# RWKV-7 decode states in a one-core hybrid decoder step: the sample's state update in transposed form

## The chip, the cores and the metric

The kernel runs on one NeuronCore of a Trainium2 chip. The metric is the device time of one execution in microseconds (us). PE is the matrix engine, PEld its weight loads, DVE the vector engine, ACT the scalar engine, POOL the general-purpose engine (which also issues stores and gathers), SP the engine that issues most loads.

## What is computed

One layer of a decoder works on a prompt (1 x 512 tokens) and on a sample group (8 sequences of 4 new tokens). A projection `z = RMSNorm(x) @ W_in` is cut into an RWKV-7 group (4 heads of 64), an attention group with forget gates (FoX, 8 heads, for the sample over 2048 paged tokens of the past) and a convolution group. Their outputs go through `W_out`, then come a cross attention and a feed-forward part. The RWKV group carries a state S per sequence and head (64 x 64, value v by key k); for the sample it is read, stepped four times and written back as `s_rwkv`:

```
def step(S, inp):
    r_t, w_t, k_t, v_t, kk_t, a_t = inp
    sa = jnp.einsum('bhvk,bhk->bhv', S, -kk_t)
    S = S * w_t[:, :, None, :] + sa[..., None] * (kk_t * a_t)[:, :, None, :] + v_t[..., None] * k_t[:, :, None, :]
    return S, jnp.einsum('bhvk,bhk->bhv', S, r_t)
```

## The kernel before

The kernel is one program of unrolled instructions. It is written as Python generators whose steps are woven by assumed costs (`woven`, L330); a scheduler then orders the instructions of every engine at build time, by data, by free buffers and by place in the program. `tc.high_priority(800)` moves what is issued under it 800 places ahead. An engine runs its list strictly in that order.

Up to about 320 us of the span three streams are woven (L1244): `fox_and_conv`, the rest of the input projection (products of 128x128 weights with 272 columns in fp32r, three per weight block, into `bank_g`); `rwkv_recurrence`, urgent by 800 (L1243); and `conv_ahead`. The first of them ends the stretch; what is left of the others is issued in `rest` (L1583), which goes on with `recurrence_end` (L1281: two ACT passes, then L1286 and L1287 on POOL, over the RWKV output), the prompt's attention, the memory keys and values, and the output projection of the prompt. Beside `rest` runs `sample_past` (L1708), the attention of the sample over its past: for every sequence four gathers of keys (1 MB each, issued by POOL), transposed by DVE (L1407) into `KT`, and four gathers of values into `page`.

`sample_steps` (L968) is the last part of `rwkv_recurrence`. It works on 32 sample tokens per head (8 sequences by 4), which lie on 32 partitions per head (`po`), while keys and values of a head lie on 64 partitions (`ro`):

- L969 to L979: the state is loaded with v on the partitions (two loads of 256 KB), then turned to k on the partitions (`S0T`) by 32 products with the identity. A float32 product is two PE instructions, a transposition (`tr`, L214) one.
- L983 to L988: `TKs` gets the token-major forms of four sources (`beta`, `kap`, `zv`, `e3s`) by 16 products.
- L989 to L1031: the small triangular systems of the four steps, and the products of `S0T` with r and kk (L1017), 512 columns wide on 64 rows. They end in the updated values `Un` (L1033).
- L1034 to L1048: the output y, its group norm, its transposition (L1045) and the sum into `ynT`, which `recurrence_end` takes.
- L1051 to L1067: the new state in the first orientation. POOL spreads three rows of `TKs` over the 8 sequences (L1054, in `two`, which takes the place of `S0T`, and `sel_t`). For each of two j, and each of its two heads, three products of 32 rows by 64 weights by 512 columns follow: `Un` by spread keys, `TKs[.., 2]` by spread keys, and ones by the spread decay (`e3s`), the last to copy the decay to all rows of v. DVE adds and multiplies from PSUM (L1064, L1065), and two stores of 256 KB leave by POOL.

All PSUM tiles of this part come from `rb(k)` (L373), three banks with one buffer each: a tile on bank k waits until the last one there has been read. The prompt's attention takes the same three banks (`xb`, L1253) afterwards.

Of the kernel before, what the change touches and what calls it, by code (L numbers as in the profile page):

```python
# [8 lines left out]
F32 = mybir.dt.float32  # L9
# [11 lines left out]
NB = 8  # L21
TS = 4
# [132 lines left out]
def hybrid_step(tc, A):  # L155
# [20 lines left out]
    def acopy(out, in_):  # L176
        nc.scalar.copy(out, in_)  # L177
# [7 lines left out]
    def mm(out, lhsT, rhs, start=True, stop=True):  # L185
        pinned(nc.tensor.matmul(out, lhsT, rhs, start=start, stop=stop, skip_group_check=True))  # L186
# [9 lines left out]
    def C(name, lo=0, n=None):  # L196
        o, w = _CF[name]
        o -= 128
        return cf[:, o + lo: o + (w if n is None else lo + n)]
# [309 lines left out]
    for h4 in range(2):  # L509
        ps = xb()  # L510
# [385 lines left out]
    def rwkv_recurrence():  # L896
# [71 lines left out]
        def sample_steps(rk, rk2):  # L968
            S0 = rk.tile([128, 2, NB, 64], F32, name="S0")  # L969
            for j in range(2):  # L970
                load(out=S0[:, j], in_=A["state_rwkv"][0, :, 2 * j: 2 * j + 2].rearrange("b r v k -> (r v) b k"))
            S0T = rk.tile([128, 2, NB, 64], F32, name="S0T")
            for j in range(2):
                ps = rb(j)
                for b in range(NB):
                    for r in range(2):
                        ro = HALF[r]
                        mm(ps[ro, b * 64: b * 64 + 64], S0[ro, j, b], ident[ro, ro])
                acopy(S0T[:, j], ps.rearrange("p (b v) -> p b v", v=64))  # L979
# [3 lines left out]
            TKs = rk.tile([128, 4, 64], F32, name="TKs")  # L983
            ps = rb(2)
            for n, src in enumerate((beta, kap, zv, None)):
                for h, j, po, ro in HR:
                    mm(ps[po, n * 64: n * 64 + 64], e3s[ro, j] if src is None else src[ro, j, sm], ident[ro, ro])
            acopy(TKs, ps[:, :256].rearrange("p (n v) -> p n v", v=64))  # L988
# [36 lines left out]
            for h, j, po, ro in HR:  # L1025
                mm(ps[po, 0:64], GS[po, 96:128], TKs[po, 2])
            rhs = rk.tile([128, 64], F32, name="rhs")
            vtt(out=rhs, in0=ps[:, 0:64], in1=sel[0], op=ADD)
            for h, j, po, ro in HR:
                mm(ps[po, 64:128], RS[po], rhs[po])  # L1030
            yield 2.0  # L1031
            Un = rk.tile([128, 64], F32, name="Un")
            vcp(Un, ps[:, 64:128])  # L1033
            for h, j, po, ro in HR:  # L1034
                mm(ps[po, 128:192], GS[po, 0:32], Un[po], True, False)
            for h, j, po, ro in HR:
                mm(ps[po, 128:192], GS[po, 64:96], TKs[po, 2], False, True)
# [13 lines left out]
            two = rk.tile([128, 2, NB, 64], F32, name="S0T")  # L1051
            ex = [two[:, 0], two[:, 1], rk2.tile([128, NB, 64], F32, name="sel_t")]
            for n, (src, m) in enumerate(((0, "own"), (1, "own"), (3, "last"))):
                ptt(out=ex[n], in0=TKs[:, src, None, :].broadcast_to([128, NB, 64]), in1=C(m)[:, :, None].broadcast_to([128, NB, 64]), op=MUL)  # L1054
            for j in range(2):
                ps, ps2 = rb(0), rb(1)
                for r in range(2):
                    h = 2 * j + r
                    po, ro = HR[h][2], HR[h][3]
                    mm(ps[ro, :], Un[po], ex[0][po], True, False)  # L1060
                    mm(ps[ro, :], TKs[po, 2], ex[1][po], False, True)
                    mm(ps2[ro, :], ones[po, :64], ex[2][po])
                S0j = S0[:, j].rearrange("p b k -> p (b k)")
                vtt(out=S0j, in0=ps, in1=S0j, op=ADD)  # L1064
                vtt(out=S0j, in0=ps2, in1=S0j, op=MUL)  # L1065
            for j in range(2):
                store(out=A["s_rwkv"][0, :, 2 * j: 2 * j + 2].rearrange("b r v k -> (r v) b k"), in_=S0[:, j])  # L1067

# [1133 lines left out]
```

## Time and profile before

| what | us |
|---|---|
| runs of the kernel | 1249.62, 1257.96, 1259.0; median 1257.96 |
| the profiled execution | 1254.13 |
| its span, first to last instruction | 1252.2 |
| mean granted clock of PE | 0.959 of full |

The profile gives one execution. The span leaves out 1.9 us at the ends. Times in the rows are microseconds from the span's start where not marked ns. PEclk is the clock granted to PE as a share of full speed (1.00 is 2.4 GHz, 0.50 is 1.2 GHz). In rows of instructions, "32*64 32x512" is a weight of 32 rows and 64 columns with 512 columns streamed, and "x8" a count.

### The profile page before, as it was taken

Reading aid. Unit: us, or ns where it says so; the run is one execution under the profiler, and the core shown is the slowest. Engines: PE = TensorE matmul, PEld = TensorE weight load, DVE = VectorE, ACT = ScalarE, POOL = GpSimd, SP = SyncE. Lnnn points to the kernel's source line nnn. Section 1 sums busy time; section 2 is a strip of 40 time slices with the busy share of each in tenths; the row PEclk is TensorE's granted clock in tenths of the full one; section 3 lists DMA queues with packets and bytes.
Section 4 is the critical chain, followed back from the end, with each engine's and each line's share of the span. In section 5 each row is a group of like instructions: output and inputs, shape, how many; then the busy total and the mean of one; then the engine's idle time right before and its main releaser. Section 6 shows DMA issues by size and latency. Waiting matters only on the chain.

```text
span 1252.2 us, 24836 instructions
## 1 busy us (share of the span) xinstructions
PE 1162.3 (93%) x10410; PEld 996.7 (80%) x10410; DVE 808.3 (65%) x1516; ACT 500.2 (40%) x994; POOL 288.4 (23%) x322
## 2 busy tenths in 40 slices
PE   6889989999899998988989879999999999999997
PEld 6788878884655566775569756999999999999996
DVE  4798998865578666783345766567777325767522
ACT  5454543341346553432433333254444223444321
POOL 1252430132533322312322330031111001111120
PEclk9999999997688998989989999999999999999998
DMA  7222220131677799979425462232321332322241
GB/s 236 62 68 53 52 77 2 54 94 39 204 288 282 273 338 360 336 257 304 169 91 161 131 247 72 77 121 70 100 91 57 97 91 95 102 90 70 81 126 35
DMA packets 129650, 173.83 MB, mean 139 GB/s; under 512 B 7030, under 2 KB 110982, under 8 KB 121337
## 3 DMA queue, kind: packets, MB, share of 16 engines
q1 hardware_dynamic: 88160, 70.76, 18.6%
q0 software_dynamic: 15216, 84.80, 18.5%
q10 hardware_dynamic: 26160, 16.66, 4.7%
q8 instruction: 82, 1.34, 0.5%
q14 instruction: 32, 0.25, 0.1%
HBM read 164.54 MB, written 7.88 MB: 138 GB/s over the span
## 4 chain that ended last, share of the span: by engine, by line
PE 46%; issue 7%; DVE 4%; DMA 3%; ACT 2%; POOL 1%; POOLq 0%; DVEq 0%; ACTq 0%
PE bank_g L186 33%; PE bank_d L186 7%; PE bank_s L186 2%; PE bank_a L186 2%; PE bank_v L186 1%; DMA page<-in_cache_fox_v_dram,kidx 1%; PE bank_t L216 1%; DVE w_lo L247 1%; DMA w_raw<-in_cache_fox_k_dram,kidx 1%; ACT w_hi L177 1%; DVE KT L1407 1%; DMA w_raw<-in_w_xq_dram 0%; DMA w_raw<-in_w_xo_dram 0%; DVE four L1649 0%; PE bank_r L186 0%
## 5 line engine op out<-in xcount | busy, mean ns | idle before, releaser
L186 PE MATMUL bank_g<-four,w_hi 128*128 128x272 f32 (+1 forms) x1536 | 278.0, 299 | 4.9 <-ACT w_hi L177 4.3
L177 ACT CAST w_hi<-w_raw 128x1024 fp32r<-128x1024 f32 (+3 forms) x149 | 140.5, 946 | 264.2 <-PE bank_g L186 189.2
L186 PEld LDWEIGHTS bank_g<-four,w_hi 128*128 128x128 f32 x1536 | 222.1, 189 | 14.5 <-issue 5.1
L247 DVE TENSOR_TENSOR w_lo<-w_raw,w_hi 128x1024 fp32r<-128x1024 f32 (+3 forms) x149 | 163.6, 1099 | 81.8 <-ACT w_hi L177 74.2
L186 PE MATMUL bank_g<-four,w_lo 128*128 128x272 f32 (+1 forms) x768 | 172.0, 299 | 0.0
L186 PE MATMUL bank_g<-act_h,w_hi 128*128 128x272 f32 (+2 forms) x400 | 123.8, 309 | 5.9 <-ACT w_hi L177 2.0
L186 PEld LDWEIGHTS bank_g<-four,w_lo 128*128 128x128 f32 x768 | 122.0, 189 | 5.5 <-issue 2.9
L186 PE MATMUL bank_g<-act_l,w_hi 128*128 128x272 f32 (+2 forms) x400 | 121.1, 303 | 0.0
L186 PE MATMUL bank_g<-act_h,w_lo 128*128 128x272 f32 (+2 forms) x400 | 120.8, 302 | 0.0
L2113 POOL TENSOR_SCALAR ysm<-HS,vec 128x32 f32<-128x32 f32 x44 | 42.0, 955 | 255.1 <-ACT HS L177 255.1
L186 PEld LDWEIGHTS bank_g<-act_h,w_hi 128*128 128x128 f32 x400 | 78.4, 196 | 11.5 <-issue 3.8
L186 PEld LDWEIGHTS bank_g<-act_l,w_hi 128*128 128x128 f32 x400 | 78.5, 196 | 2.7 <-issue 1.2
L1407 DVE STREAM_TRANSPOSE KT<-w_raw 128x2048 f32<-128x2048 f32 x32 | 73.6, 2301 | 10.9 <-DMA w_raw<-in_cache_fox_k_dram,kidx 9.9
L186 PEld LDWEIGHTS bank_g<-act_h,w_lo 128*128 128x128 f32 x400 | 78.0, 195 | 1.3 <-issue 0.2
L186 PE MATMUL bank_d<-four,w_hi 128*128 128x272 f32 x384 | 78.4, 300 | 0.0
L186 PE MATMUL bank_g<-in_h,w_hi 128*128 128x272 f32 x352 | 73.5, 290 | 0.0
L186 PE MATMUL bank_g<-in_l,w_hi 128*128 128x272 f32 x352 | 73.5, 290 | 0.0
L186 PE MATMUL bank_g<-in_h,w_lo 128*128 128x272 f32 x352 | 73.4, 289 | 0.0
L186 PEld LDWEIGHTS bank_d<-four,w_hi 128*128 128x128 f32 x384 | 62.1, 193 | 0.9
L2105 DVE TENSOR_TENSOR up<-bank_g,tot 128x544 f32<-128x544 f32 x44 | 31.8, 722 | 44.3 <-PE bank_g L186 44.3
L186 PE MATMUL bank_d<-four,w_lo 128*128 128x272 f32 x192 | 56.8, 296 | 0.0
L1392 POOL DMA_INDIRECT w_raw<-in_cache_fox_k_dram,kidx x32 | 34.2, 1069 | 97.1 <-DVE KT L1407 64.1
(632 smaller groups left out, 2425.7 us busy)
## 6 DMA issues: line engine op xcount, KB each, us to landing
w_raw<-in_w_up_dram SPq DMA_DIRECT2D x20, 1024.0 KB
w_raw<-in_w_down_dram SPq DMA_DIRECT2D x16, 704.0 KB
w_raw<-in_w_in_dram SPq DMA_DIRECT2D x17, 512.0 KB
w_raw<-in_cache_mem_k_dram SPq DMA_DIRECT2D x16, 512.0 KB
sV<-in_cache_mem_v_dram POOLq DMA_DIRECT2D x12, 512.0 KB
w_raw<-in_w_in_dram SPq DMA_DIRECT2D x4, 1024.0 KB
w_raw<-in_w_xk_dram ACTq DMA_DIRECT2D x8, 512.0 KB
w_raw<-in_w_xv_dram ACTq DMA_DIRECT2D x8, 512.0 KB
```

What stands on the lines that cost most here:

```text
L177: nc.scalar.copy(out, in_)
L186: pinned(nc.tensor.matmul(out, lhsT, rhs, start=start, stop=stop, skip_group_check=True))
L216: pinned(nc.tensor.transpose(out=out, in_=in_, identity=ident[p0:p0 + k, p0:p0 + k]))
L247: tt(out=l, in0=src, in1=h.bitcast(F32), op=SUB)
L1392: nc.gpsimd.indirect_dma_start(out=t, out_offset=None, in_=A[cache][0].rearrange("n (k j) h d -> (n k) (j h d)", j=4), in_offset=bass.Indi ...
L1407: nc.vector.transpose(out=KT, in_=K)
L2105: vtt(out=two(x[:, 2:]), in0=ev2(ps), in1=two(rstd), op=MUL)
L2113: nc.gpsimd.tensor_scalar(out=ysm, in0=H[:, 2:6, 1:], scalar1=w[2], scalar2=b, op0=MUL, op1=ADD)
```

## The change

The state stays in the transposed form `S0T` (k on the partitions) until the end. The loads bring two sequences side by side on the partitions, four heads along the free axis, so that 8 transpositions of 128x128 replace the 32 products. `TKs` holds v, and beneath each other beta (32 rows) and kap (32 rows) for two heads. `Un` and v are built a second time, beneath each other in the same order (`below`), and spread over the sequences by DVE (`ex`). One product of 64 rows by 64 weights by 512 columns per head, four in all, then gives the sum of both outer products. DVE adds it to `S0T` and multiplies by the decay, which in this orientation is a number per partition and sequence, straight from `e3s`. Eight transpositions and two ACT copies bring the state back, and 8 stores of 64 KB write it.

```diff
         def sample_steps(rk, rk2):
-            S0 = rk.tile([128, 2, NB, 64], F32, name="S0")
-            for j in range(2):
-                load(out=S0[:, j], in_=A["state_rwkv"][0, :, 2 * j: 2 * j + 2].rearrange("b r v k -> (r v) b k"))
+            S0 = rk.tile([128, 4, 256], F32, name="S0")
+            for b in range(NB):
+                load(out=S0[HALF[b % 2], b // 2].rearrange("p (h k) -> p h k", k=64), in_=A["state_rwkv"][0, b].rearrange("h v k -> v h k"))
             S0T = rk.tile([128, 2, NB, 64], F32, name="S0T")
             for j in range(2):
                 ps = rb(j)
-                for b in range(NB):
-                    for r in range(2):
-                        ro = HALF[r]
-                        mm(ps[ro, b * 64: b * 64 + 64], S0[ro, j, b], ident[ro, ro])
+                for n in range(4):
+                    tr(ps[:, n * 128: (n + 1) * 128], S0[:, n, j * 128: (j + 1) * 128])
                 acopy(S0T[:, j], ps.rearrange("p (b v) -> p b v", v=64))
...
-            TKs = rk.tile([128, 4, 64], F32, name="TKs")
+            TKs = rk.tile([128, 3, 64], F32, name="TKs")
             ps = rb(2)
-            for n, src in enumerate((beta, kap, zv, None)):
-                for h, j, po, ro in HR:
-                    mm(ps[po, n * 64: n * 64 + 64], e3s[ro, j] if src is None else src[ro, j, sm], ident[ro, ro])
-            acopy(TKs, ps[:, :256].rearrange("p (n v) -> p n v", v=64))
+            for h, j, po, ro in HR:
+                mm(ps[po, 0:64], zv[ro, j, sm], ident[ro, ro])
+            acopy(TKs[:, 0], ps[:, :64])
+            ps = rb(1)
+            for j in range(2):
+                for n, src in enumerate((beta, kap)):
+                    for r, ro in enumerate(HALF):
+                        mm(ps[64 * r + 32 * n: 64 * r + 32 * n + 32, j * 64: 64 + j * 64], src[ro, j, sm], ident[ro, ro])
+            acopy(TKs[:, 1:], ps[:, :128].rearrange("p (n v) -> p n v", v=64))
...
             for h, j, po, ro in HR:
                 mm(ps[po, 64:128], RS[po], rhs[po])
+            below = [rb(2), rb(0)]
+            for h, j, po, ro in HR:
+                mm(below[j][ro.start + 32: ro.stop, :64], zv[ro, j, sm], ident[ro, ro])
+                mm(below[j][ro.start: ro.start + 32, :64], RS[po], rhs[po])
             yield 2.0
             Un = rk.tile([128, 64], F32, name="Un")
             vcp(Un, ps[:, 64:128])
+            ex = [rk2.tile([128, NB, 64], F32, name="sel_t") for _ in range(2)]
+            for j in range(2):
+                vtt(out=ex[j], in0=below[j][:, None, :64].broadcast_to([128, NB, 64]),
+                    in1=C("own")[:, :, None].broadcast_to([128, NB, 64]), op=MUL)
...
-            two = rk.tile([128, 2, NB, 64], F32, name="S0T")
-            ex = [two[:, 0], two[:, 1], rk2.tile([128, NB, 64], F32, name="sel_t")]
-            for n, (src, m) in enumerate(((0, "own"), (1, "own"), (3, "last"))):
-                ptt(out=ex[n], in0=TKs[:, src, None, :].broadcast_to([128, NB, 64]), in1=C(m)[:, :, None].broadcast_to([128, NB, 64]), op=MUL)
+            both = [rb(2), rb(0)]
             for j in range(2):
-                ps, ps2 = rb(0), rb(1)
-                for r in range(2):
-                    h = 2 * j + r
-                    po, ro = HR[h][2], HR[h][3]
-                    mm(ps[ro, :], Un[po], ex[0][po], True, False)
-                    mm(ps[ro, :], TKs[po, 2], ex[1][po], False, True)
-                    mm(ps2[ro, :], ones[po, :64], ex[2][po])
-                S0j = S0[:, j].rearrange("p b k -> p (b k)")
-                vtt(out=S0j, in0=ps, in1=S0j, op=ADD)
-                vtt(out=S0j, in0=ps2, in1=S0j, op=MUL)
+                for ro in HALF:
+                    mm(both[j][ro, :], TKs[ro, 1 + j], ex[j][ro])
             for j in range(2):
-                store(out=A["s_rwkv"][0, :, 2 * j: 2 * j + 2].rearrange("b r v k -> (r v) b k"), in_=S0[:, j])
+                new = S0T[:, j]
+                vtt(out=new, in0=both[j].rearrange("p (b v) -> p b v", v=64), in1=new, op=ADD)
+                vtt(out=new, in0=new, in1=e3s[:, j, TS - 1:: TS, None].broadcast_to([128, NB, 64]), op=MUL)
+            yield 1.0
+            for j in range(2):
+                ps = rb(2 * j)
+                for n in range(4):
+                    tr(ps[:, n * 128: (n + 1) * 128], S0T[:, j, 2 * n: 2 * n + 2].rearrange("p b v -> p (b v)"))
+                acopy(S0[:, :, j * 128: (j + 1) * 128], ps.rearrange("p (n c) -> p n c", c=128))
+            for b in range(NB):
+                store(out=A["s_rwkv"][0, b].rearrange("h v k -> v h k"), in_=S0[HALF[b % 2], b // 2].rearrange("p (h k) -> p h k", k=64))
```

`TKs[po, 2]` becomes `TKs[po, 0]` where v is read for rhs and y.

## Rows read from the trace of the kernel before

**Rows 1.** The page, part 1: busy us, share, instructions of PE.

```profile
PE 1162.3 (93%) x10410; PEld 996.7 (80%) x10410; DVE 808.3 (65%) x1516; ACT 500.2 (40%) x994; POOL 288.4 (23%) x322
```

**Rows 2.** Stages: length, busy PE, PEld, DVE, ACT, POOL, PEclk, DMA, GB/s.

```profile
278.50:289.00 10.50, 10.50 (x122) 5.41 (x122) 8.77 (x14) 3.87 (x8) 5.93 (x5) 1.00 0.30 102
294.40:301.50 7.10, 7.10 (x24) 1.61 (x20) 1.91 (x5) 0.00 (x0) 0.00 (x0) 0.66 0.00 0
301.50:303.40 1.90, 1.90 (x10) 1.64 (x8) 1.41 (x6) 0.29 (x2) 0.00 (x0) 0.50 0.00 0
303.40:311.50 8.10, 8.10 (x18) 2.18 (x18) 2.28 (x7) 0.67 (x3) 0.99 (x1) 0.50 0.14 33
311.50:319.60 8.10, 8.10 (x42) 7.48 (x41) 2.98 (x5) 3.62 (x7) 2.91 (x2) 0.65 0.14 32
319.60:323.20 3.60, 1.10 (x10) 0.77 (x9) 3.57 (x8) 0.00 (x0) 3.46 (x3) 1.00 0.59 183
323.20:330.00 6.80, 6.69 (x22) 3.71 (x22) 5.77 (x19) 2.68 (x10) 4.23 (x8) 0.56 0.88 293
```

**Rows 3.** The chain that ended last: start us, length us, what.

```profile
505.32 9.05 DMA w_raw<-in_cache_fox_k_dram,kidx
...
573.35 8.93 DMA page<-in_cache_fox_v_dram,kidx
```

**Rows 4.** Stages, `S0T` alone: length, PE, PEld, ACT, POOL, PEclk, DMA, GB/s.

```profile
294.40:301.50 7.10, 6.06 (x8) 0.94 (x8) 0.00 (x0) 0.00 (x0) 0.66 0.00 0
...
303.40:311.50 8.10, 6.46 (x8) 1.47 (x8) 0.00 (x0) 0.00 (x0) 0.50 0.14 33
```

**Rows 5.** PE groups, 270.9 to 294.2 us: busy us, mean ns of one.

```profile
L186 PE MATMUL bank_r<-S0T,RA 64*32 64x512 f32 x16 | 5.2, 601 | 0.0
L186 PE MATMUL bank_r<-ident,S 64*64 64x64 f32 x64 | 3.1, 225 | 0.0
...
L186 PE MATMUL bank_r<-rhs,RS 32*32 32x64 f32 x8 | 0.3, 226 | 0.0
...
L186 PE MATMUL bank_r<-ident,e3s 64*32 64x64 f32 x8 | 0.3, 216 | 0.0
```

**Rows 6.** Timeline of PE: start us, length us, instructions merged, idle before.

```profile
283.00 1.05 PE L186 MATMUL bank_r<-S0T,RA 64*32 64x512 f32 x4
...
297.02 1.96 PE L186 MATMUL bank_r<-S0T,Un 32*64 32x512 f32 x2
...
319.56 0.49 PE L186 MATMUL bank_r<-four 64*128 64x128 f32 x4
...
323.23 0.66 PE L216 MATMUL bank_x<-ident,four 128*128 128x128 f32 x4 [2.53 <-DVE four L794]
```

**Rows 7.** Timeline of DVE: start us, length us, instruction.

```profile
287.81 0.69 DVE L1019 TENSOR_TENSOR sel_t<-bank_r,cf 128x512 f32<-128x512 f32 x1 [0.30 <-PE bank_r L186]
...
301.27 0.69 DVE L1064 TENSOR_TENSOR S<-bank_r,S 128x512 f32<-128x512 f32 x1 [5.16 <-PE bank_r L186]
```

**Rows 8.** Timeline of POOL: start us, length us, instructions, idle before.

```profile
271.09 0.69 POOL L1235 DMA_DIRECT2D out_dram<-gn_y  x1
...
289.09 2.05 POOL L1054 TENSOR_TENSOR S0T<-TKs,cf 128x512 f32<-128x512 f32 x2 [2.29 <-PE bank_r L186]
...
306.42 0.99 POOL L1067 DMA_DIRECT2D out_dram<-S  x1 [14.28 <-DVE rsq L233]
...
319.77 2.85 POOL L1287 TENSOR_TENSOR four<-zb 128x1088 f32<-128x1088 f32 x1
...
332.69 2.09 POOL L1402 TENSOR_TENSOR w_hi<-qrep,cpf 128x512 f32<-128x512 f32 x2 [3.71 <-issue]
```

**Rows 9.** Timeline of ACT: start us, length us, instruction.

```profile
284.57 0.59 ACT L177 COPY S0T<-bank_r 128x512 f32<-128x512 f32 x1 [1.90 <-PE bank_r L186]
```

**Rows 10.** Timeline of SP, which issues the state's loads.

```profile
252.48 1.94 SPq L971 DMA_DIRECT2D S<-in_state_rwkv_dram  x2
```

More of the change, by code (lines that the diff above doesn't have):

```diff
@@ L1025, in sample_steps @@
             for h, j, po, ro in HR:
-                mm(ps[po, 0:64], GS[po, 96:128], TKs[po, 2])
+                mm(ps[po, 0:64], GS[po, 96:128], TKs[po, 0])
             rhs = rk.tile([128, 64], F32, name="rhs")
@@ L1036, in sample_steps @@
             for h, j, po, ro in HR:
-                mm(ps[po, 128:192], GS[po, 64:96], TKs[po, 2], False, True)
+                mm(ps[po, 128:192], GS[po, 64:96], TKs[po, 0], False, True)
             ys = rk.tile([128, 64], F32, name="ys")
```

## The prediction

> **What bounds the kernel now.** I read the page's busy times first, then the span cut into stages, then the rows of the stage that the change touches, and last what starts behind it. PE is busy 1162.3 of 1252.2 us [rows 1], so in most of the span a microsecond taken from PE is one taken from the end. Whether that holds at this place the stages must say. From 278.5 to 319.6 us PE has no gap at all: busy equals length in each stage [rows 2]. The sample's RWKV steps and the last input projections share it there. The steps are urgent, so they go first and the projections fill what is left, until the last projection ends at 319.5 and the attention's first products start, at 319.56 [rows 6].
>
> So this stretch is bound by PE's work, not by its waits, and two things in it stand out. From 294.4 to 311.5 PE is busy 17.1 us, of which only 1.9 hold projections. And PEclk is 1.00 up to 289, 0.66 in the stage from 294.4, 0.50 to 311.5 and 0.65 in the stage after it [rows 2]: the clock falls from 2.4 to 1.2 GHz while PE is fully busy, in the middle of products of 32 rows; two of them take 1.96 us there [rows 6]. It recovers some way into the projections that follow.
>
> What comes behind, up to about 650 us, is the attention over the past. The chain that ended last runs there through waits for gathers, such as 9.05 and 8.93 us [rows 3]. These gathers take the buffers that the same stage frees, so a stage that begins earlier also gathers earlier; I take it that the whole rest moves with the end of the projections.
>
> **The change, part by part.** All of it is against the profiled execution: span 1252.2, time 1254.1, which is 3.8 below the median of the runs, 1257.96.
>
> Removed, the old update. In the first stage the products with `S0T` (by this name the spread keys) cover 6.06 us [rows 4]; the rest of that stage is y. From 303.4 to 311.5 nothing but update products runs, so all 8.10 us count [rows 2]. Together 14.2 us.
>
> Added, the new update: 4 products, 8 instructions of 64 rows by 64 weights by 512 columns. The nearest row is the product of `S0T` with r and kk, 64 rows by 32 weights by 512 columns, four instructions in 1.05 us [rows 6]: heads on different halves of the rows run at once. So 2 x 1.05 = 2.1 us. The other end is 1.96 us for two, one after the other at half clock, as the old ones: 7.8 us. I take 2.1, because the halves are laid out as in the nearer row.
>
> One rule of the Trainium skill speaks against that: TensorEngine Tiling (Array Packing), Gotcha 1, says that different row tiles cannot access the same PSUM bank at the same time, and the two heads of a j here share a bank. By it the two would go one behind the other, and the sum would be some 2 us smaller. The products with r and kk also write one bank from both halves, and 1.05 us for four with 0.6 us for one [rows 5, 6] shows them side by side, so the trace does not agree with it for this layout.
>
> The state's first turn: 64 instructions, 3.1 us [rows 5], become 8 transpositions; four take 0.66 us [rows 6], so 1.3. Saved 1.8. The last turn adds another 8: 1.3 us.
>
> `TKs` loses one source of four, 8 instructions or 0.3 us. `below` adds 16 small ones, of the kinds that take 0.3 us for eight [rows 5]: 0.6. Net 0.3 us more.
>
> The clock. If the narrow products were what brought it down, it stays up. At half clock were about 0.7 us of y in the first stage, the 1.90 us of the second, and of the 8.1 us at 0.65 the part (1 - 0.65) / 0.5, which is 5.7 us [rows 2]. Half of these 8.3 us comes back: 4.1 us. The other end is 0. I take 4.1, since the 10.5 us from 278.5 to 289, full of products on 64 rows, kept 1.00 [rows 2].
>
> A rule bears on this one too. The Trainium skill, TensorE: Matmul & The Clock Gate, section "HAM oscillation", puts such falls down to idle gaps between bursts of products. Here the clock fell with PE busy 7.10 of 7.10 us, so the trace does not agree that a gap is needed. By the rule alone the new stretch, without gaps too, keeps its clock, and the sum is the same.
>
> PE in all: 14.2 + 1.8 + 4.1 - 2.1 - 1.3 - 0.3 = 16.4 us less before the attention starts.
>
> Given back. The four DVE operations on the state, 0.69 us each [rows 7], stood in a stretch where DVE had time (it waited 5.16 us for the first). With the projections ending near 303 they fall into the place where DVE is busy 3.57 of 3.6 us and PE waits 2.53 us for it [rows 2, 6]; they are urgent, so the last key block's normalisation queues behind them. I charge their 2.8 us. Below it could be 0, if they come earlier; above, 4.2, if the two spreads (`ex`, now on DVE, 0.69 each) land there too. The multiplication by a broadcast decay is not in the trace; the 0.69 of the spread with a broadcast operand is the nearest.
>
> POOL loses three spreads of 1.0 us and gets 8 stores for 2. A store of the same form, 64 partitions by four runs, took 0.69 us, the old one 0.99 [rows 8]: 5.5 for 1.9, 3.6 us more. Behind them may stand L1286 and L1287, and behind these the first keys' preparation L1402, before which POOL waited 3.71 us [rows 8]. That wait covers it barely: I charge 1.0, ends 0 and 3.6.
>
> The banks. `both` takes bank 2 after y's transposition has been read, and the attention's first tiles take the same three banks after the state's last copy. I charge one copy, 0.6 us [rows 9]; the ends are 0 and 7.4, the whole of that tail uncovered (2.1 + 2.8 + 1.3 + two copies of 0.59).
>
> The 8 loads cost SP about what 2 cost, some 2 to 8 us from 252 [rows 10], by 0.97 us each at most; the state is first read at 278.5, so nothing.
>
> Sum: 16.4 - 2.8 - 1.0 - 0.6 = 12.0 us. 1254.1 - 12.0 = 1242.1 for a profiled execution, and 1258.0 - 12.0 = **1246.0 us** against the median of the runs.
>
> **The rivals.**
> 1. Nothing is given back. DVE's share comes early, since `ex` needs only `below` and DVE is busy 1.91 of 7.10 us there [rows 2], and the attention's start waits for other things. Then 16.4 us: 1241.6. Against it stands only the full DVE at 319.6.
> 2. The clock falls all the same: the small products of y and `below` on 32 rows are still there, and less filler stands between them. The gain loses 4.1, pays 2.1 more for the update and 1.3 for the last turn: 12.0 - 7.5 = 4.5, or 1253.5. For it: 0.56 in the stage from 323.2, where PE is busy 6.69 of 6.80 us [rows 2], so little is needed. Against it: 1.00 before 289.
> 3. The tail becomes the bound: the update can't start until y has left bank 2, the projections have run out, and the attention waits for the banks. Of the 7.4 us of tail, 0.6 is charged; if 5 more show, the gain is 7 us: 1251.0.
> 4. Slower. The eight stores and the later L1287 stand before the gathers in POOL's order; a key gather slips behind the transposition that should have hidden it, and DVE waits for it as in the 9.05 us row [rows 3]. One such wait eats most of the gain; from the second on the kernel is slower: -12 + 2 x 9 = 6, or 1264. For it: POOL is in order, and the static list of the whole attention is drawn up anew. Against it: the first gathers were issued before this stretch ends, and the stores cost 3.6 us once, not per sequence.
>
> The change does what it says: the count of products goes from 24 instructions to 8 by the code alone, so a rival of no effect on PE I leave out.
>
> **How the numbers follow.** Chances: forecast 0.42, rival 1 0.22, rival 2 0.20, rival 3 0.11, rival 4 0.05. One per cent, about what a measurement of this kernel can tell from no change, is 12.6 us, almost exactly the forecast's gain. Its own range is a gain of 8 to 17 us (1241 to 1250) and just under half of it lies beyond 12.6: 0.20. With rival 1 that is faster by over 1%: 0.42. The other part of the forecast, 0.22, with rivals 2 and 3 is within 1%: 0.53. Rival 4 is slower: 0.05. The range goes from 1236 (all of 16.4, and some 5 us more from a better order behind) to 1259 (the clock falls, the update runs one product behind the other); it leaves out the second wait of rival 4.
>
> **What would show it.** Right: between the last small product before `Un` and the attention's first product PE takes some 16 us less; eight 64x512 instructions on `S0T`'s update in about 2.1 us; PEclk near 1.00 up to the attention; L1287 ending a few us after the projections, as now. A PEclk of 0.5 with 3.4 us or more for those eight would be rival 2; PE idle longer than 2.53 us at the attention's start, ended by the copies of the state, rival 3; a new wait for a gather, rival 4. The forecast is wrong if the attention starts 12 us earlier and the end does not: then the stage behind does not move with its start.

## The result, and the profile after

The changed kernel took 1263.37 us (median of 17 executions, 1256.94 to 1271.24) against 1255.65 us for the kernel before (17 executions, 1249.62 to 1260.31): a ratio of 1.0056, 95% interval 1.0037 to 1.0076. It is half a per cent slower where I had forecast 1246.0 and a gain of 12 us. Measured a second time, beside other kernels, it came to 1258.89 us and a ratio of 1.0008 (0.9981 to 1.0036). By the two intervals it lies between 0.2% faster and 0.8% slower; a gain of 12 us there is not. The profiled execution took 1268.53 us, its span is 1266.8, and it lies 5.2 above its median where that of the kernel before lies 1.5 below: the two profiles are 14.4 us apart, the two medians 7.7.

The work did go. The page of the changed kernel, part 1, the row of PE (to be read against [rows 1]):

```profile
PE 1155.7 (91%) x10354; PEld 992.1 (78%) x10354; DVE 807.1 (64%) x1513; ACT 502.5 (40%) x1002; POOL 287.0 (23%) x325
```

PE is busy 6.6 us less, and yet the span is 14.6 us longer: the gain was turned into waiting. The stages of [rows 2], of the kernel after (length, busy PE, PEld, DVE, ACT, POOL, PEclk, DMA, GB/s):

```profile
278.50:289.00 10.50, 9.09 (x74) 8.18 (x75) 5.83 (x8) 4.46 (x10) 4.27 (x4) 1.00 0.30 107
294.40:301.50 7.10, 7.10 (x35) 3.19 (x35) 1.97 (x7) 0.00 (x0) 0.00 (x0) 0.50 0.00 0
301.50:303.40 1.90, 1.90 (x15) 1.42 (x7) 1.14 (x2) 0.00 (x0) 0.00 (x0) 0.50 0.00 0
303.40:311.50 8.10, 8.10 (x59) 5.37 (x58) 3.34 (x10) 2.38 (x5) 0.00 (x0) 0.50 0.01 3
311.50:319.60 8.10, 6.94 (x37) 4.18 (x36) 5.92 (x20) 1.31 (x5) 2.17 (x3) 0.83 0.35 94
319.60:323.20 3.60, 1.65 (x13) 1.27 (x12) 3.32 (x4) 1.22 (x2) 3.46 (x6) 1.00 1.02 396
323.20:330.00 6.80, 2.62 (x79) 2.19 (x77) 5.21 (x10) 3.31 (x8) 5.42 (x9) 0.85 0.55 146
```

The clock did not stay up. It is at half for the 17 us from 294.4 on, worse than before, and from 319.6 PE has little to do. PE's own timeline says what came ahead of the fall (start, length, instructions merged, idle before):

```profile
288.30 1.11 PE L186 MATMUL bank_r<-S0T,RA 64*32 64x512 f32 x6 [1.41 <-ACT S0T L177]
...
293.90 0.42 PE L186 MATMUL bank_r<-ident,zb 64*32 64x64 f32 x2 [3.24 <-DVE sel_t L1024]
...
311.51 1.97 PE L186 MATMUL bank_r<-sel_t,TKs 64*64 64x512 f32 x4
...
318.94 1.08 PE L186 MATMUL bank_r<-sel_t,TKs 64*64 64x512 f32 x4 [0.43 <-DVE yT L1061]
```

The row at 293.90 is the first product of `below`. It needs only `zv` and bank 2, so the scheduler put it early in PE's order, ahead of projections that were ready; bank 2 was still being read by DVE (L1024), and DVE was late, behind the convolution's rows. PE stood for 3.24 us with projections queued behind. The last row is the second half of the update: it comes 7 us behind the first, because it waits until y's transposition has left bank 2.

So the state's tail falls behind the projections' end (315.70, where SP's load of `cpf`, L1366, is released; 319.53 before). POOL's timeline shows what that tail stands in front of, and one row of DVE what waits for it:

```profile
322.06 2.11 POOL L1299 TENSOR_TENSOR zb<-zb 128x1088 f32<-128x1088 f32 x1
325.54 4.95 POOL L1080 DMA_DIRECT2D out_dram<-S  x8 [1.38 <-ACT S L177]
330.50 1.08 POOL L1415 TENSOR_TENSOR w_hi<-qrep,cpf 128x512 f32<-128x512 f32 x1
331.75 1.16 POOL L1405 DMA_INDIRECT w_raw<-in_cache_fox_k_dram,kidx  x1 [0.17 <-issue]
...
332.23 0.29 DVE L1315 CUSTOM_DVE_ANT_0 S<-bank_r,tri 128x128 f32<-128x128 f32 x1 [1.36 <-DMA out_dram<-S]
```

The eight stores hold POOL 4.95 us after a wait of 1.38, and the keys' gathers queue behind them. The prompt attention's `S`, a tile in the memory that the sample's states had, waits for the stores too.

Further behind, the chain that ended last (start, length, what) runs through loads, as [rows 3] did, but longer ones:

```profile
387.81 10.11 DMA w_raw<-in_cache_fox_k_dram,kidx
...
470.78 12.37 DMA w_raw<-in_w_xk_dram
...
502.98 9.88 DMA w_raw<-in_cache_fox_k_dram,kidx
...
561.36 19.30 DMA w_raw<-in_w_out_dram
```

The last of these is not in the chain of the kernel before. It is the first load of the output weights, and PE is busy 18.2 us of the 30 from 570 to 600 (26.2 before).

### The profile page after: what moved, and what is told of

It is laid out like the page before. It is cut to its first block, busy times and chain, and to the rows that moved or that the text cites. A ratio compares the mean times of both kernels' runs of the same rounds, so it can differ in the third digit from the quotient of the medians.

```text
span 1266.8 us, 24762 instructions
## 1 busy us (share of the span) xinstructions
PE 1155.7 (91%) x10354; PEld 992.1 (78%) x10354; DVE 807.1 (64%) x1513; ACT 502.5 (40%) x1002; POOL 287.0 (23%) x325
## 3 DMA queue, kind: packets, MB, share of 16 engines
q0 software_dynamic: 15312, 84.80, 18.2%
## 4 chain that ended last, share of the span: by engine, by line
PE 53%; DMA 6%; issue 6%; DVE 4%; ACT 3%; POOL 1%; POOLq 0%; DVEq 0%; ACTq 0%
PE bank_g L186 34%; PE bank_d L186 7%; PE bank_s L186 3%; DMA w_raw<-in_cache_fox_k_dram,kidx 3%; PE bank_a L186 2%; PE bank_r L186 2%; PE bank_v L186 2%; DVE KT L1420 2%; DMA w_raw<-in_w_out_dram 2%; PE bank_t L216 1%; DMA w_raw<-in_w_xk_dram 1%; PE bank_r L216 1%; DMA page<-in_cache_fox_v_dram,kidx 1%; DVE w_lo L247 1%; ACT w_lo L1456 1%
## 5 line engine op out<-in xcount | busy, mean ns | idle before, releaser
L186 PE MATMUL bank_g<-four,w_hi 128*128 128x272 f32 (+1 forms) x1536 | 276.3, 298 | 13.4 <-ACT w_hi L177 12.8
L186 PE MATMUL bank_s<-KT,w_hi 128*32 128x128 f32 x1024 | 44.0, 300 | 18.5 <-DVE KT L1420 6.6
L186 PEld LDWEIGHTS bank_s<-KT,w_hi 128*32 128x32 f32 x1024 | 32.2, 119 | 31.8 <-issue 10.2
```

## The experiments

Three theories at the start. T1: the local gain is real, but the static order of the whole stage behind was drawn anew, and that order loses it. T2: the new tail, POOL's stores above all, costs by itself. T3: the loss is the clock that falls behind the wait at 293.9. Two came up on the way. T4: what is lost behind is lost at the first load of the output weights. T5: the length of the fall differs between executions.

All ratios are to the kernel before in the same set of runs, since the sets ran on different chips and the kernel before had medians from 1249.0 to 1258.9 us in them. The table has one profiled execution each, with these marks: XS, the transpositions of `XS` at about 270, ahead of everything that the change touches (the same 127 product instructions into `bank_g` follow it in every profile); the projections' end (the load of `cpf`); the first transposition of keys; the first product of the next stage. "Changed again" is the second measurement of the same kernel. H, W and S are edits shown below: products held in place, output weights early, stores on SyncE.

| kernel | ratio (95%) | XS | proj. end | first keys | next stage | span |
|---|---|---|---|---|---|---|
| before | 1 | 269.9 | 319.5 | 329.2 | 650.9 | 1252.2 |
| changed | 1.0056 (1.0037–1.0076) | 272.2 | 315.7 | 321.4 | 662.6 | 1266.8 |
| changed again | 1.0008 (0.9981–1.0036) | 272.2 | 309.5 | 315.4 | 652.6 | 1256.4 |
| before + yield | 0.9994 (0.9966–1.0022) | 269.9 | 317.9 | 328.4 | 653.3 | 1257.2 |
| changed − yield | 1.0143 (1.0108–1.0178) | 274.3 | 310.8 | 316.6 | 667.3 | 1268.4 |
| H | 1.0002 (0.9978–1.0025) | 269.3 | 306.2 | 311.9 | 649.8 | 1253.3 |
| S | 1.0003 (0.9979–1.0027) | 270.5 | 312.6 | 318.3 | 658.5 | 1259.2 |
| W | 1.0003 (0.9974–1.0032) | 267.9 | 304.6 | 310.5 | 645.1 | 1248.3 |
| before + W | 1.0004 (0.9972–1.0037) | 271.0 | 319.1 | 330.4 | 652.3 | 1253.5 |
| HW | 0.9958 (0.9923–0.9992) | 271.1 | 307.5 | 313.2 | 645.3 | 1248.0 |
| HS | 0.9912 (0.9881–0.9942) | 271.9 | 312.0 | 317.7 | 645.8 | 1250.7 |
| WS | 0.9932 (0.9905–0.9958) | 271.7 | 308.2 | 314.1 | 645.8 | 1249.9 |
| HWS | 0.9875 (0.9845–0.9906) | 269.4 | 308.9 | 314.6 | 641.6 | 1240.8 |
| HW, stores on ScalarE | 0.9884 (0.9851–0.9917) | 272.6 | 309.9 | 315.6 | 641.5 | 1245.5 |
| HW, stores late on POOL | 1.0246 (1.0220–1.0273) | 270.9 | 307.0 | 312.7 | 684.1 | 1287.2 |
| old front | 1.0022 (0.9990–1.0053) | 271.0 | 305.9 | 310.8 | 654.6 | 1258.2 |
| old front, W | 0.9978 (0.9956–0.9999) | 272.1 | 305.3 | 310.2 | 644.8 | 1246.1 |
| old front, WS | 0.9931 (0.9904–0.9958) | 267.9 | 302.9 | 307.8 | 642.0 | 1243.1 |
| old front, HWS | 0.9923 (0.9897–0.9948) | 273.0 | 310.1 | 315.0 | 639.5 | 1240.5 |

**Does an order alone cost time?** One line that does no work is added to the kernel before:

```
+            yield 1.0
             for j in range(2):
                 store(out=A["s_rwkv"][0, :, 2 * j: ...
```

> The kernel before, with one added line that does no work: a yield of 1.0 ahead of the two stores of the sample's state. It only shifts where the weaving of the streams goes on, and so redraws the static order behind the state. Theory T1 (the stage behind the update got another order, and an order is worth some us either way): the end lies 3 to 12 us away from the kernel before, in a direction that can't be foretold, while the projections' end stays where it was (319.5 within 2 us) and the difference arises behind 340. T2 (the loss is the new tail: eight stores on POOL, 4.95 us, and the attention's tile that waits for them) and T3 (the loss is the fallen clock between 294 and 311): the time stays within 2 us of the kernel before, since neither is in it.

Measured: 0.9994. T1 was wrong on this one; the order behind was drawn anew, and came out as good. The same in the changed kernel, where the line that the change added is taken out:

```
                 vtt(out=new, in0=new, in1=e3s[...], op=MUL)
-            yield 1.0
             for j in range(2):
```

> The changed kernel without the yield of 1.0 that it added between the multiplication and the last transpositions. No instruction goes. T1: the projections' end stays near 315.7, the first transposition of keys near 321.4 (both within 3 us), and the end moves by 3 to 12 us from the changed kernel, direction open. T2 and T3: stores, waits and clock are as in the changed kernel, so the time stays within 2 us of it.

Measured: 1.0143, 1272.91 us; with no instruction taken away the ratio is 0.0087 above that of the changed kernel in its first measurement and 0.0135 above the second. Its projections end 36.5 us behind XS, 7 us sooner than in the changed kernel's first profile (43.5) and about as in its second (37.4), so T1's marks near the update were off; and the next stage starts 4.7 us later than in the first profile. This much an order can do, and neither T2 nor T3 has it.

**The product that was moved onto a busy bank (H).**

```
             below = [rb(2), rb(0)]
+            pin[0] = True
             for h, j, po, ro in HR:
                 mm(below[j][...], zv[ro, j, sm], ident[ro, ro])
                 mm(below[j][...], RS[po], rhs[po])
+            pin[0] = False
```

> The changed kernel with the products for the stacked values held in TensorE's order where they are written, behind the products of RS and rhs. T3: the wait of 3.24 us at 293.9 goes, the granted clock from 294 to 311 is near 1.0 in place of 0.50, the projections' end comes 8 to 12 us earlier (315.7 to about 305) and the time is 8 to 12 us shorter than the changed kernel's. T1: the local gain is there in full or part (3 to 12 us at the projections' end), but the end doesn't follow it one for one: it differs from it by 3 to 12 us either way, as the order behind is drawn anew. T2: the local end moves, the attention's S tile still waits for the eight stores, and less than half of the local gain is left at the end.

Measured: 1.0002. The projections' end comes 36.9 us behind XS, 12.7 sooner than before, but not for T3's reason: the wait for bank 2 gave way to one of 3.41 us for `GS` (DVE, L1002) at the same place, and PEclk is 0.64 and 0.83 in the two stages from 289.0 and 294.4. So H moves the wait and does not remove it, and no run with the new front tests T3. And the next stage starts at 649.8, only 1.1 us before that of the kernel before: of 13 us at the projections 1 is left 340 us later. T1 and T2 had both forecast such a loss. ACT's timeline of this kernel shows where some of it goes:

```profile
549.30 0.41 ACTq L279 DMA_DIRECT2D w_raw<-in_w_out_dram  x1
569.17 1.04 ACT L177 CAST w_hi<-w_raw 128x1024 fp32r<-128x1024 f32 x1 [16.01 <-DMA w_raw<-in_w_out_dram]
```

In the kernel before the same load is issued at 544.91 and read at 553.12:

```profile
553.12 1.04 ACT L177 CAST w_hi<-w_raw 128x1024 fp32r<-128x1024 f32 x1 [6.08 <-DMA w_raw<-in_w_out_dram]
```

With H it is issued just as the last keys' buffers come free, together with 1 MB of cross-attention weights, 1.5 MB of output weights for the sample, a store of 1 MB, and three values' gathers. It takes 20 us. It is issued late because its buffer held the first block of tokens, and the second half of that block's transposition stands behind the last batch's scores in PE's order.

**The stores on another queue (S).**

```
-                store(out=A["s_rwkv"][0, b]...
+                load(out=A["s_rwkv"][0, b]...        (load: SyncE's queue)
```

> The changed kernel with the eight stores of the state issued by SyncE's queue instead of POOL's. T2: POOL is free of 4.95 us ahead of the first masked query and of the second gather, those two come 4 to 5 us earlier, and the time falls by 3 to 7 us. T1: the first masked query comes up to 5 us earlier too, but the end moves by an amount of its own, between 10 us less and 10 us more, without relation to it. T3: clock as before, end within 2 us of the changed kernel.

Measured: 1256.83 us, 1.0003. The third keys' gather comes 12.2 us behind the projections' end, in place of 16.0; these 3.8 us are near the 4 to 5 of T2. The time is 6.5 us below the changed kernel's first median, T2's 3 to 7, but by the ratio of its second measurement (1.0008) it is only 0.6 us; this run alone does not decide.

**The old front with the new update.** Two loads and 32 products in place of eight loads and eight transpositions.

> The changed kernel with the loading and turning of the states put back (two transfers, 32 products of 64x64, in place of eight transfers and eight transpositions); the new update and the new stores stay. It asks what the new front alone is worth at the projections' end, counted from the transpositions of XS before it: changed kernel 59.0 us (256.7 to 315.7), kernel before 64.7. My prediction had the new front 1.8 us shorter: then the distance grows to about 61. If the front's transpositions only fill gaps between projections, or wait there, it stays within 1 us of 59 or falls. T1: the end of the kernel follows neither; it lies 3 to 12 us away from the changed kernel, direction open. T2, T3: the end moves by what the projections' end moves, within 2 us.

Measured: 1.0022. The distances in this expectation start at another product of `XS`, not at the transpositions that it names; counted from those, at 270, they are 49.6 (before), 43.5 and 37.4 (changed, two executions) and 34.9 here. It falls, though the span is 6.0 longer than before. Its stages from 289 on (length, PE, PEclk, DMA, GB/s):

```profile
289.00:294.40 5.40, 5.40 (x60) 1.00 0.00 0
294.40:303.00 8.60, 8.60 (x86) 1.00 0.01 2
303.00:311.50 8.50, 7.41 (x54) 1.00 0.36 113
```

and half of the update on PE's timeline:

```profile
299.34 1.07 PE L186 MATMUL bank_r<-sel_t,TKs 64*64 64x512 f32 x4
```

No gap, a full clock, and four instructions of the update in 1.07 us: that is the stretch as I had forecast it, from a front that I had called 1.8 us slower. PE's longest wait near the update is 2.08 us here, at 282.5 for the copy of `S0T`, and PEclk is 0.84 in the stage from 278.5. With the full clock from 289 on the kernel is still no faster than before, so T3 can't be the whole loss.

**The output weights earlier (W).** The first tokens' turning and the first output weights' load get priority, in the kernel with H, in the kernel before, and in the changed kernel.

```
+            with tc.high_priority(200 if i == 0 else 0):
                 for q in range(2):
                     ...  tr(ps[...], x[...]); anycp(xTs[q]...)
...
+        with tc.high_priority(200):
+            one = weights(A["w_out"][0], 8, EIGHT[:1], raws=outW)
-        yield from gemm_steps(A["w_out"][0], ..., raws=outW)
+        yield from gemm_steps(A["w_out"][0], ..., raws=outW, first=one)
```

> The kernel with the products for the stacked values held in place (first transposition of keys 17 us earlier than before, end no earlier), with one change far behind: the turning of the first block of tokens and the first output weights' load are given priority, so that TensorE's order has that turning ahead of the scores of the last batch and not behind them. TensorE's order ahead of that point is the same instruction for instruction. Theory T4, a sharper T1 (the lead is lost at about 550, where the first output weights wait 20 us because their buffer is freed behind the last scores, just as two cross-attention weights, two output weights and the values' gathers are released too): the load is issued some 8 us earlier, its wait falls from 19.9 us to under 8, the next stage's first product comes at 636 to 643 in place of 649.8, and the kernel takes 1243 to 1249. If the values' gathers set the stage's end by themselves, that wait shrinks but the next stage begins at 648 or later and the time stays within 2 us of 1255.7.

> The kernel before with the same priority for the turning of the first tokens and the first output weights' load. In it that load is already issued 14 us ahead of the last keys' landing and waits 6.1 us. T4: little to win, the time stays within 3 us of the kernel before. If the priority helps by itself, whatever the update does, it is faster by as much as the changed kernel with it (5 to 12 us).

> The changed kernel with the same priority and nothing else; TensorE's order is the changed kernel's up to that point. T4: the wait of 19.3 us for the first output weights at 561 falls to under 8, the next stage begins 8 to 13 us earlier (650 to 655), and the time falls from 1263.4 to 1250 to 1256, so that the change as such is worth what the local stage gained or a little less. T2 and T3 (the loss was made near the update): at most 3 us shorter.

ACT's timeline with H and W:

```profile
542.34 2.00 ACTq L279 DMA_DIRECT2D w_raw<-in_w_out_dram  x2
549.21 1.04 ACT L177 CAST w_hi<-w_raw 128x1024 fp32r<-128x1024 f32 x1 [4.24 <-DMA w_raw<-in_w_out_dram]
```

The wait shrinks from 16.0 to 4.2 us as T4 said, and the next stage starts at 645.3, though projections end 1.3 later than with H alone: 5.8 us are won, against 7 to 14 forecast. The ratio falls by 0.0044, 5.5 us; 1252.1 us is above the 1243 to 1249 of T4. In the kernel before W does nothing (1.0004), as T4 said. In the changed kernel it gives 1.0003, from 1.0056 or 1.0008: between 0.6 and 6.7 us, so this alone doesn't decide; the load's wait there is 8.95 us (under 8 forecast), the next stage begins at 645.2 (650 to 655 forecast), and 1256.82 us is just above the 1250 to 1256 of T4.

Two marks in the traces show T4 apart from the times: the last transposition of keys and the next stage's first product. They lie 89.3 us apart in the kernel before, 95.7 to 107.8 in the seven profiles of the new update without W, and 90.3 to 97.1 in the eight with it, the late stores below left aside. In the changed kernel's first profile the lead over the kernel before is 7.8 us at the first keys, 1.0 at the last and -11.8 at the next stage: 6.8 us are lost ahead of this load and 12.8 behind. It isn't the only place: with S alone the lead falls from 10.9 to -1.2 by the last keys, and the wait for the load is only 2.10 us.

**The changed kernel again, and four combinations.**

> The changed kernel itself once more, unaltered, beside the others on the same chip. Theory T5 (the wait of 3.2 us on the bank lets the granted clock fall, and how long it stays at the lower level differs from execution to execution): the distance from XS to the projections' end is not the 59.0 us of the first profile but anything between 48 and 59, with the granted clock after the wait to match, and the time is 1263 within 2.5 us. If the first profile's 17 us at half clock belong to the order, the distance is 58 to 60 again. For T4: the next stage again begins 11 to 12 us later than before, with the wait for the first output weights of 15 us or more.

> Old front (two transfers, 32 products of 64x64), new update, and the priority for the first tokens' turning and the first output weights. T4: as the changed kernel with the priority or a little less, 1250 to 1255, since old front and new front end at the same place (50.4 us from XS to the projections' end against 48.5 and 59.0 in two executions of the new front). If the new front is worth the 1.8 us of my prediction, this one is 1 to 3 us slower than the kernel with the new front, the products held and the priority (1252.1).

> Products held in place, priority for the first output weights, and the eight stores on SyncE's queue. T2 (stores on POOL cost by themselves): 3 to 5 us less than with POOL's stores (1252.1), so 1247 to 1249. T1 and T4: the stores' place is off the path once the order behind is good; 1250 to 1255, as without.

> Old front, new update, priority for the first output weights, stores on SyncE's queue. T2: 3 to 5 us below the same kernel with POOL's stores. T1 and T4: within 3 us of it, either way.

The changed kernel's second profile has the same instructions in the same order and the same wait of 3.24 us, but another clock (length, PE, PEclk, DMA, GB/s):

```profile
289.00:294.40 5.40, 2.16 (x37) 0.93 0.02 3
294.40:303.00 8.60, 8.60 (x51) 0.65 0.00 0
303.00:311.50 8.50, 7.56 (x73) 1.00 0.13 28
```

T5 holds in this pair: 0.65 for one stage, then 1.00, where the first profile had 0.50 for two. Its projections end 6.2 us sooner, and this lead goes through: 6.0 at the first keys, 10.1 at the next stage, 10.4 in the span. With one and the same order, what was gained at the projections arrived at the end in these two executions. The rest of that expectation failed but for the wait of 17.9 us for the output weights: the time is 1258.89, not 1263 within 2.5, and the next stage begins 1.7 us behind that of the kernel before, not 11 to 12.

All three edits together: 0.9875, 1242.81 us, 14.8 below the kernel before in the same set. That is a gain of the size that was forecast for the change alone (12.0). T2 had said 3 to 5 us for S; the ratio fell by 0.0083 from HW, about 10 us, and with the old front by 0.0047, about 6 us: more than forecast, and against T1 and T4, which had it off the path. The old front with W is 0.0020 above HW; it lacks H, so that run does not tell the fronts apart.

POOL's timeline with HW (stores on POOL):

```profile
317.67 1.03 POOL L1407 DMA_INDIRECT w_raw<-in_cache_fox_k_dram,kidx  x1 [0.30 <-issue]
321.12 4.40 POOL L1082 DMA_DIRECT2D out_dram<-S  x7 [2.42 <-ACT S L177]
325.68 0.63 POOL L1082 DMA_DIRECT2D out_dram<-S  x1 [0.16 <-issue]
326.62 1.09 POOL L1407 DMA_INDIRECT w_raw<-in_cache_fox_k_dram,kidx  x1 [0.30 <-issue]
```

and with HWS:

```profile
319.10 1.02 POOL L1407 DMA_INDIRECT w_raw<-in_cache_fox_k_dram,kidx  x1 [0.30 <-issue]
320.42 1.00 POOL L1407 DMA_INDIRECT w_raw<-in_cache_fox_k_dram,kidx  x1 [0.30 <-DVE Sn L1400]
```

Two gathers lie 8.95 us apart in the one and 1.32 in the other: POOL stood for the copy of the states and for its own stores.

**POOL's cost or a lucky order?**

> As the fastest kernel so far (products held, output weights early, stores on SyncE: 1242.8, ratio 0.9875), but the eight stores issued by ScalarE's queue. T2 (POOL's 5 us in front of the gathers are the cost): the third and fourth keys' gathers come as early as with SyncE (10 to 12 us behind the projections' end), and the ratio is 0.985 to 0.991. T1 (only a lucky order): the order is drawn once more, and the ratio lies anywhere between 0.985 and 1.000, more likely near the 0.9958 of POOL's stores than near 0.9875.

> Products held and stores on SyncE, without the priority for the output weights. T2 and T4 together (each of the two costs its own part): slower than the kernel with all three by what the priority gave elsewhere (ratio 0.0044), so 0.990 to 0.994, with a wait of 15 us or more for the first output weights at 540 to 560. T1: any ratio from 0.988 to 1.005.

> Stores on SyncE and output weights early, the products where the scheduler had put them. T3: the bank's wait of 3.2 us and the fallen clock behind it are there, so it is 3 to 8 us slower than with the products held (1246 to 1251, ratio 0.991 to 0.995). If the hoisted products cost nothing, it is 1241 to 1245.

With the stores on ScalarE's queue: 0.9884, and gathers 10.2 and 11.5 us behind the projections' end, as T2 said. But PE's order is that of HWS, so it was not drawn once more: the run shows that the two queues are alike, and does not part T2 from T1. HS came to 0.9912, as T2 with T4 had said, with 19 us from the issue of the output weights' load to its use (546.1 to 565.2). WS came to 0.9932, inside T3's range, but not for T3's reason: HWS has a wait of 3.42 us and a fallen clock too (0.86 and 0.69 in the two stages from 289.0 and 294.4), and its projections end later behind XS than those of WS (39.6 and 36.5 us). Taken from the table, S is worth 0.003 to 0.009 wherever it is added, W 0.003 to 0.007 (between WS and S it is 0.0071), H 0.003 to 0.009, if 1.0032, the mean of the two measurements, stands for the changed kernel. By the intervals each of these differences is uncertain by 0.004 or so. S moves more than the stores: PE's order between 320 and 554 us is another in HWS than in HW. No single pair can tell POOL's time from that order; that all five pairs gain with S speaks for T2.

**The same stores on POOL, but later.**

```
+            with tc.high_priority(-1200):
                 for b in range(NB):
                     store(out=A["s_rwkv"][0, b]...
```

> Products held, output weights early, the eight stores again on POOL, but with a low priority: in POOL's order they stand one or two at a time behind the third to tenth key gathers, not as a block ahead of the fourth. If their place costs, the third and fourth keys' gathers come 9 to 12 us behind the projections' end, as with SyncE, and the ratio is 0.985 to 0.991. If POOL's 5 us cost wherever they stand, it stays at 0.994 to 0.998 as with the block (0.9958).

Measured: 1.0246, 1288.98 us. The gathers are as early as with SyncE (10.2 and 11.5 us), and still it is the slowest of all. POOL's last stores and DVE's first addition into the prompt attention's `S`:

```profile
397.49 2.58 POOL L1083 DMA_DIRECT2D out_dram<-S  x4
...
406.64 0.29 DVE L1318 CUSTOM_DVE_ANT_0 S<-bank_r,tri 128x128 f32<-128x128 f32 x1
```

With HW that addition is at 329.99. The attention's tiles lie in the states' memory, as the changed kernel's wait for `out_dram<-S` at 332.23 shows; that the late start comes from the late stores is inferred from this, since the row at 406.64 shows no wait. From 330 to 420 PE is busy 52.6 of 90 us (83.8 with HW). Both forecasts of this run failed: the gathers' lead was there and the time was not. Stores behind the gathers cost more than stores ahead of them; neither place that was tried on POOL is as good as another queue.

**Does H gain by itself?** With the old front PE's order with and without H differs in 34 rows near the update and nowhere behind.

> Old front, new update, products held, output weights early, stores on SyncE. TensorE's order differs from the kernel with the old front and without the hold (ratio 0.9931) in 34 rows near the update and nowhere behind. If the hold gains by itself, 3 us or more: ratio 0.987 to 0.991. If its gain elsewhere came through the order behind, it stays within 2 us: 0.9915 to 0.9947. The distance from XS to the projections' end stays at 47 to 51 us, with the clock at 1.00 up to 311, as in the three kernels with the old front.

Measured: 0.9923 against 0.9931, no gain. With the old front PE does not wait for bank 2, so H had nothing to remove there; that its gain in the other kernels came through the order behind fits this, but is not shown. The distance (52.6 us by the mark of the expectation) and the clock were not as expected: PEclk is 0.59 in the stage from 289.0, and ahead of it PE has a longer wait than in the other three kernels with the old front (at most 2.08 us):

```profile
287.57 1.06 PE L186 MATMUL bank_r<-S0T,RA 64*32 64x512 f32 x2 [3.11 <-ACT S0T L177]
```

## Why the prediction was wrong

**The terms of PE's work held.** Eight instructions of the update take 2.1 us at full clock, as charged (in the changed kernel's first profile 1.97 and 1.08, the first four partly at half clock); the first turn takes 1.5 us in eight transpositions (1.3 charged, 3.1 before), the last turn 1.2 (1.3 charged). The old update's 14.2 us are gone. The Trainium skill's rule on row tiles that share a bank (TensorEngine Tiling (Array Packing), Gotcha 1), weighed there, would have given two instructions one after the other. The trace does not agree: 1.07 us for four, two heads on one bank, where one of the products with r and kk takes 0.6 [rows 5], says again that they run side by side.

**The end of the stretch moved by less than 16.4.** From XS to the projections' end it is 48.0 to 49.6 us in the three profiles with the old update, 36.1 to 43.5 (mean 38.3) in twelve with the new one and the new front, 33.2 to 37.1 in four with the old front. So 10 us on average, 13.5 with the old front. Without the clock's 4.1, and less a new wait of 3.3, the 16.4 would leave 9.0 (an estimate from these rows). In the three kernels with the old front and no wait over 2.1 us it is 14.2, and 16.4 less the first turn's 1.8 is 14.6: there the local sum came out within 0.4 us. At the end of the stretch the first turn's "saved 1.8" has the wrong sign: 1.6 shorter on PE, but both copies of `S0T` ran together at 287.7, where the kernel before had the second at 284.57 [rows 9], and the products behind them met DVE while it worked off the convolution.

**The clock's +4.1 failed in most executions.** I had argued from a stretch without gaps. The new stretch has one, 3.2 to 3.4 us in all twelve profiles with the new front, and in the lower of the two stages from 289.0 and 294.4 PEclk is 0.50 to 0.80. A full clock from 289 to 303 was seen only in three of the four kernels with the old front; the fourth is the one with the wait of 3.11 us. In the kernel before the clock fell with PE busy throughout (0.50 with 8.10 of 8.10 us [rows 2]). The Trainium skill, TensorE: Matmul & The Clock Gate, section "HAM oscillation", has idle gaps as the cause. The trace of the changed kernel agrees (3.24 us, then 0.50), that of the kernel before does not; by that rule, read against the new order and not against the old, rival 2 would have been the better forecast for the clock.

**The step that failed: "I take it that the whole rest moves with the end of the projections".** It held where the order behind stayed (6.2 us at the projections, 10.4 at the end, in two executions of one order). The change drew that order anew for 330 us, and the wait for the output weights' load grew in it from 6.1 us to 18. In the changed kernel's first profile a lead of 7.8 us at the first keys is a lag of 11.8 at the next stage; in the second, 13.8 is a lag of 1.7. The prediction had named the sign of it, "if the attention starts 12 us earlier and the end does not".

**POOL's "I charge 1.0" was mis-sized**, and rival 4 had the right mechanism at a chance of 0.05: "the eight stores and the later L1287 stand before the gathers in POOL's order". Its price, 1264, was near, though partly by luck: it counted two waits for gathers, and what the runs show is 0.003 to 0.009 for the stores (4 to 11 us) and 0.003 to 0.007 for the output weights' load (4 to 9 us), which no rival had. The 3.71 us of POOL's waiting that were to cover the stores [rows 8] were not there any more: L1415 follows the stores at once. Of the 2.8 us charged to DVE half shows in the changed kernel: two of the four operations on the state (320.06 and 320.79, 0.69 us each) stand right ahead of the first keys' transposition at 321.39. Rival 3's tail is there as well: the states' last copy comes 9 us behind the projections' end, because half of the update waits for y to leave bank 2.

**What stays open.** Which place in the order gave H its 0.003 to 0.009 with the new front was not traced. Whether the gap at 289 can be closed with the new front was not tried, so what the fallen clock costs at the end is open too. How much of S is POOL's own time and how much the order that came with it is not parted.

## What to carry to other kernels

Where a static order is drawn by a scheduler, price an edit in two parts: what it takes from the bounding engine, up to a mark that you can read (here the projections' end), and whether the transfers behind that mark are still issued ahead of the waits that they have to hide; the second part can eat the first whole: the three edits, most of whose worth lay there, took the changed kernel's ratio from 1.0008 or 1.0056 to 0.9875, some 17 to 23 us. Put added stores on a queue that has nothing behind them, and look up whose tiles take the memory that they leave. When a gain does not show, compare the marks between the two traces and look at the first one where the lead shrinks, before the change itself is blamed.

## What was not expected of the hardware

The same instructions in the same order, with the same wait of 3.24 us, got half the clock for 17 us in one execution and a mean of 0.65 for 8.6 us in another; the projections' end moved by 6 us with it, and the end of the span by 10. Eight stores cost their issuing engine 0.62 us each on POOL (4.95 us) and 0.69 to 0.73 on SyncE and ScalarE (5.53 us with HWS, 5.82 with the stores on ScalarE): the queue is no cheaper, but there no gather of keys stands behind the stores.
